# Rotary embedding on one Trainium2 core: sine and cosine products of both halves in one VectorE instruction each, and a shorter f32 tail on SyncE's queue

## Chip, cores, metric

One core of a Trainium2 chip. The metric is the device time of one execution, in us; the median of several executions is quoted. Single runs of one kernel scatter by some 0.1 to 0.3 us (a few lay 0.3 to 0.5 us above the median), so differences under 0.1 us are not read as differences. The experiments were run in five sets, each on one chip with the kernel before beside it: e1 to e4, e5 to e8, a1 to a4, f1 to f4, g1 and g2. The profiled executions quoted here were all fast, granted clock 1.0. A ratio is the mean time of one kernel's fast runs over that of the other's fast runs of the same rounds; it is therefore not quite the ratio of the medians. "The span" is from the profile's first instruction to its last; the time is some 1.8 us longer.

## The reference

```python
# x: (8, 8, 1024, 64) f32, freqs: (32,) f32, positions: (1024,) int32
half = x.shape[-1] // 2
angles = np.outer(positions, freqs)
cos, sin = np.cos(angles), np.sin(angles)
x_first, x_second = x[..., :half], x[..., half:]
out_first = x_first * cos - x_second * sin
out_second = x_first * sin + x_second * cos
```

In all 16.8 MB of f32 are read and 16.8 MB of f32 written.

## The kernel before

x is cut into eight tiles of 128 partitions x 64 rows x 64 columns. GpSimd's queue (q0 in the profile) loads them, f32 to bf16, all but the first 16 rows of the first tile, which SyncE's queue (q1) loads; later q0 stores each result, bf16 to f32. The last 24 rows of the last tile are computed straight to f32 and stored by q1 in three pieces of eight rows, so that the end of the program does not hang on q0 alone.

```python
for g in range(ntiles):                         # all loads are queued at the start
    lo = 0 if g else head
    nc.gpsimd.dma_start(out=xts[g][:, lo:], in_=hbm(x, g, lo))
# ... angles, sin_h and cos_h as bf16 [128, 64, 32] (cut) ...

def rotate(g, lo, hi, ot):
    xf = xts[g][:, lo:hi, :half];  xs = xts[g][:, lo:hi, half:]
    of = ot[:, :, :half];          os_ = ot[:, :, half:]
    sin = sin_h[:, lo:hi];         cos = cos_h[:, lo:hi]
    t1 = tpool.tile([P, C, half], bf16, name="t1")[:, :hi - lo]
    t2 = tpool.tile([P, C, half], bf16, name="t2")[:, :hi - lo]
    v.tensor_mul(out=t1, in0=xf, in1=sin)
    v.tensor_mul(out=t2, in0=xs, in1=sin)
    v.tensor_mul(out=of, in0=xf, in1=cos)
    v.tensor_mul(out=os_, in0=xs, in1=cos)
    v.tensor_sub(out=of, in0=of, in1=t2)
    v.tensor_add(out=os_, in0=os_, in1=t1)

tail = 3 * piece                                # piece = 8 rows
for g in [1, 0] + list(range(2, ntiles)):       # eight bf16 tiles, the last one without its tail
    hi = C if g < ntiles - 1 else C - tail
    ot = opool.tile([P, C, d], bf16, name="ot")[:, :hi]
    rotate(g, 0, hi, ot)
    ots.append(ot)
    nc.gpsimd.dma_start(out=hbm(out, g, 0, hi), in_=ot)
last = singles.tile([P, tail, d], f32)
rotate(ntiles - 1, C - tail, C, last)

for done in [pos_i, fr, x0] + ots[:-1]:         # SyncE waits here until each store but the last has landed
    sp.clobber_nop(outs=[sp.lower_ap(done)])
for r in range(0, tail, piece):                 # then issues the tail
    lo = C - tail + r
    tc.keep_in_program_order(
        sp.dma_start(out=hbm(out, ntiles - 1, lo, lo + piece), in_=last[:, r:r + piece]))
sp.clobber_nop(outs=[sp.lower_ap(ots[-1])])     # and waits for the last store
# ... and for the tail's pieces (cut) ...
```

## Time and profile before

| | before |
|---|---|
| time, median of the rounds with the changed kernel | 85.25 us |
| span | 83.6 us |
| VectorE busy | 63.5 us in 66 instructions |
| VectorE's last instruction ends | 73.7 us |
| tile 6 landed, tail issued | 77.8 us |
| first tail packet on q1 | 79.44 us |
| last landing on q0, on q1 | 80.80, 82.69 us |

The table reads from top to bottom in time: VectorE is done ten microseconds before the end, and what follows is waiting for bytes. The last two rows come from the trace's records of DMA packets and landings. The prediction shows the lines that this rests on.

### The profile page before, as it was taken

How to read it: one execution, taken by the hardware profiler on the slowest of the kernel's cores; microseconds unless marked ns; L12 is line 12 of the kernel's file. 1: busy time of each engine (PE TensorE's matmuls, PEld its weight loads, DVE VectorE, ACT ScalarE, POOL GpSimd, SP SyncE). 2: the span in 40 equal slices, each digit the busy share in tenths (PEclk: the TensorE clock that was granted, in tenths of full speed). 3: DMA queues.
4: the chain of work that ended last, by engine and by line, in shares of the span. 5: the costliest groups of instructions: out<-in, count | busy, mean ns of one | idle time of the engine just before them, and what ended most of it. 6: DMA issues, size and time to landing. Idle time of an engine off the chain costs nothing.

```text
span 83.6 us, 163 instructions
## 1 busy us (share of the span) xinstructions
DVE 63.5 (76%) x66; ACT 9.3 (11%) x6; POOL 8.7 (10%) x20
## 2 busy tenths in 40 slices
DVE  1024995089999999999999999999999999920000
ACT  0000049999000000000000000000000000000000
POOL 4960000000002001002002002000100202000000
DMA  0899999999999999999999999999999999999992
GB/s 0 182 202 259 227 208 227 204 227 208 212 220 208 227 208 227 204 212 223 200 388 423 423 455 400 470 388 463 408 439 439 416 455 423 455 392 422 431 331 70
DMA packets 3065, 25.45 MB, mean 304 GB/s; under 512 B 360, under 2 KB 376, under 8 KB 1144
## 3 DMA queue, kind: packets, MB, share of 16 engines
q0 software_dynamic: 2304, 24.12, 94.2%
q1 hardware_dynamic: 720, 1.31, 5.1%
q10 hardware_dynamic: 40, 0.01, 0.0%
q14 instruction: 1, 0.01, 0.0%
HBM read 16.79 MB, written 16.78 MB: 402 GB/s over the span
## 4 chain that ended last, share of the span: by engine, by line
DVE 67%; DMA 12%; ACT 7%; DVEq 1%; SPq 1%; issue 0%; ACTq 0%
DMA x<-in_x_dram 12%; DVE t L114 11%; DVE t L115 11%; DVE ot L119 10%; DVE ot L117 10%; DVE ot L116 10%; DVE ot L118 10%; ACT sin_h L96 2%; ACT L96 2%; ACT L101 2%; ACT xt L101 1%; DVEq L170 1%; DVE last L117 1%; DVE last L118 1%; DVE last L116 1%; SPq L56 1%
## 5 line engine op out<-in xcount | busy, mean ns | idle before, releaser
L114 DVE TENSOR_TENSOR t<-xt,sin_h 128x2048 bf16<-128x2048 bf16 (+2 forms) x9 | 9.9, 1099 | 3.5 <-ACT sin_h L96 3.5
L128 POOL DMA_DIRECT2D out_dram<-ot x8 | 4.2, 526 | 60.4 <-DVE ot L119 60.4
L115 DVE TENSOR_TENSOR t<-xt,sin_h 128x2048 bf16<-128x2048 bf16 (+2 forms) x9 | 9.9, 1099 | 0.0
L117 DVE TENSOR_TENSOR ot<-xt,cos_h 128x2048 bf16<-128x2048 bf16 (+1 forms) x8 | 9.3, 1167 | 0.0
L119 DVE TENSOR_TENSOR ot<-ot,t 128x2048 bf16<-128x2048 bf16 (+1 forms) x8 | 9.3, 1167 | 0.0
L116 DVE TENSOR_TENSOR ot<-xt,cos_h 128x2048 bf16<-128x2048 bf16 (+1 forms) x8 | 9.3, 1166 | 0.0
L118 DVE TENSOR_TENSOR ot<-ot,t 128x2048 bf16<-128x2048 bf16 (+1 forms) x8 | 9.3, 1166 | 0.0
L74 POOL DMA_DIRECT2D xt<-in_x_dram x8 | 4.3, 577 | 0.8 <-PEq L170 0.8
L76 DVE LOAD_MASK_SELECT pos_i<-pos_i x1 | 0.0, 14 | 3.8 <-DMA pos_i<-in_positions_dram 3.8
L101 ACT ACT_TABLE_LOAD x1 | 1.3, 1283 | 11.5 <-DMA x<-in_x_dram 11.5
L87 DVE TENSOR_TENSOR turns<-pos_f,fturn 128x2048 f32<-128x2048 f32 x1 | 2.3, 2293 | 0.0
L93 DVE TENSOR_TENSOR turns<-turns,whole 128x2048 f32<-128x2048 f32 x1 | 2.3, 2293 | 0.0
L99 ACT ACTIVATE cos_h<-whole,half_pi 128x2048 bf16<-128x2048 f32 x1 | 2.0, 2003 | 0.0
L96 ACT ACTIVATE sin_h<-turns 128x2048 bf16<-128x2048 f32 x1 | 1.9, 1909 | 0.0
L98 ACT ACTIVATE whole<-turns 128x2048 f32<-128x2048 f32 x1 | 1.9, 1893 | 0.0
L77 DVE LOAD_MASK_SELECT fr<-fr x1 | 0.0, 14 | 1.9 <-DMA fr<-in_freqs_dram 1.9
L96 ACT ACT_TABLE_LOAD x1 | 1.3, 1283 | 0.0
L91 DVE TENSOR_SCALAR whole<-turns 128x2048 f32<-128x2048 f32 x1 | 1.2, 1226 | 0.0
L101 ACT CAST xt<-x 128x1024 bf16<-128x1024 f32 x1 | 1.0, 1045 | 0.0
L117 DVE TENSOR_TENSOR last<-xt,cos_h 128x768 f32<-128x768 bf16 x1 | 0.9, 950 | 0.0
L119 DVE TENSOR_TENSOR last<-last,t 128x768 f32<-128x768 f32 x1 | 0.9, 950 | 0.0
L116 DVE TENSOR_TENSOR last<-xt,cos_h 128x768 f32<-128x768 bf16 x1 | 0.9, 949 | 0.0
(12 smaller groups left out, 2.6 us busy)
## 6 DMA issues: line engine op xcount, KB each, us to landing
out_dram<-ot POOLq DMA_DIRECT2D x7, 2048.0 KB, 18.5
xt<-in_x_dram POOLq DMA_DIRECT2D x7, 1024.0 KB, 25.2
out_dram<-ot POOLq DMA_DIRECT2D x1, 1280.0 KB, 11.2
xt<-in_x_dram POOLq DMA_DIRECT2D x1, 768.0 KB, 7.6
out_dram<-last SPq DMA_DIRECT2D x3, 256.0 KB, 3.6
x<-in_x_dram SPq DMA_DIRECT2D x2, 256.0 KB, 6.9
pos_i<-in_positions_dram ACTq DMA_DIRECT2D x1, 8.0 KB, 3.7
fr<-in_freqs_dram ACTq DMA_DIRECT2D x1, 0.5 KB
```

What stands on the lines that cost most here:

```text
L74: nc.gpsimd.dma_start(out=xts[g][:, lo:], in_=hbm(x, g, lo))
L87: nc.vector.tensor_mul(out=turns, in0=pos_f.to_broadcast([P, C, half]), in1=fturn.to_broadcast([P, C, half]))
L93: nc.vector.tensor_sub(out=turns, in0=turns, in1=whole)
L96: nc.scalar.activation(out=sin_h, in_=turns, func=Sin, scale=twopi)
L101: nc.scalar.copy(out=xts[0][:, :head], in_=x0)
L114: v.tensor_mul(out=t1, in0=xf, in1=sin)
L115: v.tensor_mul(out=t2, in0=xs, in1=sin)
L116: v.tensor_mul(out=of, in0=xf, in1=cos)
L117: v.tensor_mul(out=os_, in0=xs, in1=cos)
L118: v.tensor_sub(out=of, in0=of, in1=t2)
L119: v.tensor_add(out=os_, in0=os_, in1=t1)
L128: nc.gpsimd.dma_start(out=hbm(out, g, 0, hi), in_=ot)
```

## The change

The intent: fewer VectorE instructions, since sine (and cosine) multiply both halves alike and can be read twice through a repeated row; and eight rows fewer for the f32 tail, whose queue was taken to be the slower one.

```diff
     def rotate(g, lo, hi, ot):
-        ... six instructions, as above ...
+        n = hi - lo
+        pair = [P, n, 2, half]
+        xt = xts[g][:, lo:hi].rearrange("p c (two h) -> p c two h", two=2)
+        ot = ot.rearrange("p c (two h) -> p c two h", two=2)
+        t = tpool.tile([P, C, 2, half], bf16, name="t")[:, :n]
+        v.tensor_mul(out=t, in0=xt, in1=sin_h[:, lo:hi, None, :].to_broadcast(pair))
+        v.tensor_mul(out=ot, in0=xt, in1=cos_h[:, lo:hi, None, :].to_broadcast(pair))
+        v.tensor_sub(out=ot[:, :, 0], in0=ot[:, :, 0], in1=t[:, :, 1])
+        v.tensor_add(out=ot[:, :, 1], in0=ot[:, :, 1], in1=t[:, :, 0])
 
-    tail = 3 * piece
+    tail = 2 * piece
 ...
-    for done in [pos_i, fr, x0] + ots[:-1]:
+    for done in [x0, pos_i, fr] + ots[:-1]:
```

## The prediction

> **What bounds the kernel now.** I read the page first, then the stretches of time, the timeline of the end, the DMA traffic of the last microseconds, and the groups of instructions by shape. The page offers two candidates: the chain that ended last gives VectorE 67% of the span, and the slices show VectorE full from 17 us to 74 us. But the DMA row under it is full for longer:
>
> ```profile
> DVE  1024995089999999999999999999999999920000
> ...
> DMA  0899999999999999999999999999999999999992
> ...
> q0 software_dynamic: 2304, 24.12, 94.2%
> q1 hardware_dynamic: 720, 1.31, 5.1%
> ...
> HBM read 16.79 MB, written 16.78 MB: 402 GB/s over the span
> ```
>
> VectorE is full in the middle only; DMA is full from the second slice to the last but one, and two queues together fill 99% of what sixteen engines have. The same by stages (columns after the stretch: length, then busy us of VectorE, ScalarE, GpSimd with instruction counts, clock, DMA share, GB/s):
>
> ```profile
> 2.00:42.00 40.00, 31.61 (x31) 9.32 (x6) 5.14 (x10) 1.00 1.02 215
> 42.00:77.80 35.80, 31.73 (x33) 0.00 (x0) 2.61 (x5) 1.00 1.06 428
> 77.80:80.40 2.60, 0.00 (x0) 0.00 (x0) 0.00 (x0) 1.00 1.04 397
> 80.40:82.40 2.00, 0.00 (x0) 0.00 (x0) 0.00 (x0) 1.00 0.73 251
> 82.40:83.60 1.20, 0.00 (x0) 0.00 (x0) 0.00 (x0) 1.00 0.00 0
> ```
>
> Until 42 us the loads run. The 215 GB/s count what lands as bf16; the f32 read from HBM is twice that, 430 GB/s. From 42 us to 77.8 us the stores run at 428 GB/s. Both are the same ceiling. Only after 80.4 us does the DMA share fall (0.73, then 0); that is the only place where time is left. The timeline says who waits for whom there:
>
> ```profile
> 65.20 0.52 POOL L128 DMA_DIRECT2D out_dram<-ot  x1 [6.29 <-DVE ot L119]
> ...
> 69.61 0.52 POOL L128 DMA_DIRECT2D out_dram<-ot  x1 [3.89 <-DVE ot L119]
> ...
> 72.78 0.95 DVE L119 TENSOR_TENSOR last<-last,t 128x768 f32<-128x768 f32 x1
> 77.84 2.27 SPq L141 DMA_DIRECT2D out_dram<-last  x3
> ```
>
> The last two bf16 stores are handed to GpSimd's queue at 65.2 and 69.6 us, but the stores move one after another, and SyncE, which waits for each to land, counts 4.8 us between them (2.1 MB in 4.8 us is again some 430 GB/s). Tile 6 lands at 77.8 us, so its bytes began near 73: about 7 us after it was ready. The last bf16 store waits 8 us. VectorE itself is done at 73.7 us, 10 us before the end of the span. The chain's 67% VectorE is therefore a chain of order, not of need. The f32 tail is ready at 73.7 us, but SyncE issues it only at 77.84 us, after its wait for tile 6. Its transfer looks like this (two stretches, 77.8 to 79.4 and 79.4 to 80.4 us):
>
> ```profile
> q0 software_dynamic: 68, 0.70, 110.5%
> ```
> ```profile
> q1 hardware_dynamic: 149, 0.28, 77.1%
> q0 software_dynamic: 21, 0.05, 17.2%
> ```
>
> For 1.6 us after the issue no tail packet moves; q0 has the engines. When q1 begins, q0 has 0.05 MB left, so almost all of the 0.79 MB tail moves alone, from 79.4 to 82.35 us: 266 GB/s, not 430. Its three pieces land 3.6 us after their issues, at 81.4, 82.1 and 82.7 us by the trace's landing records (0.63 us apart); q0's last landing is 80.8 us. The tail's third piece ends the program.
>
> **What the Trainium skill says.** (1) "VectorE: DVE Perf Modes", § The perf-mode tier table: a bf16 `tensor_tensor` runs two elements a cycle, f32 one; 1224 and 2293 ns for 2048. The trace agrees: 1217 ns and 2293 ns. (2) "Vector Engine (DVE) Microarchitecture Reference", § 5.1: the two-element mode asks for 16-bit operands and an innermost step of one, and a row read again and again with a step of 0 still ran in that mode with two sources. The strided halves, rows of 32, do run at 1217 ns here; no instruction here repeats a bf16 row. (3) "DMA: Bandwidth & Descriptors", § Where 436 GB/s comes from: 435 GB/s for one core's DMA. The trace's 428 to 430 is close to that. (4) Same page, § Queues, rings and completion order: each engine takes turns between queues, packet by packet. The trace shows both queues' packets between 79.4 and 80.4 us, too few of q0 to test it.
>
> **The change part by part.** *VectorE's instructions.* The costs come from these groups:
>
> ```profile
> L114 DVE TENSOR_TENSOR t<-xt,sin_h 128x2048 bf16<-128x2048 bf16 x7 | 8.5, 1217 | 3.5 <-ACT sin_h L96 3.5
> L116 DVE TENSOR_TENSOR last<-xt,cos_h 128x768 f32<-128x768 bf16 x1 | 0.9, 949 | 0.0
> L118 DVE TENSOR_TENSOR ot<-ot,t 128x1280 bf16<-128x1280 bf16 x1 | 0.8, 816 | 0.0
> ```
>
> Neighbours overlap by 0.08 us, so I use the steps between starts: 1.137 us at 2048 elements (six take 51.19 to 58.01), 0.735 us at 1280 (six take 64.82 to 69.23). The slope is 0.402 us over 768 = 0.523 ns an element; the fixed part 0.066 us. One f32 step at 768 is 0.87 us: (0.87 - 0.066)/768 = 1.047 ns an element.
> - Full tile: before 6 x 1.137 = 6.82 us. After: two products of 4096 at 2.21 us, add and subtract at 1.137: 6.69 us. Saved 0.13 us, two fixed parts, times seven = 0.9 us. A product should show some 2290 ns (1217 + 2048 x 0.523).
> - Last bf16 part, 48 rows in place of 40: 2 x 1.67 + 2 x 0.87 = 5.08 us, before 4.41: +0.67 us.
> - f32 tail, 16 rows in place of 24: 0.60 + 1.14 + 2 x 0.60 = 2.94 us, before 4.42 (69.23 to 73.65): -1.48 us.
> - Sum: -0.9 + 0.67 - 1.48 = -1.7 us of VectorE, which ends at 72.0 us; its instructions fall from 66 to 48. The last store is ready at 69.3 - 0.9 + 0.67 = 69.1 us.
>
> All this lies beside the DMA stream, inside 7 to 8 us of slack. On the path it is worth zero.
>
> *The split of the end.* The bytes stay the same. Eight rows (128 x 8 x 64 x 4 B = 0.262 MB) move from q1 to q0. SyncE's issue time doesn't change, since tile 6 lands as before. Bounds for the gain:
> - If the pace of the pieces sets the end, the third one's 0.63 us goes: -0.63 us.
> - If the queues' rates set it: from 79.4 us q0 has 0.05 + 0.26 = 0.31 MB at 430 GB/s, 0.73 us, then q1's 0.524 MB at 266 GB/s, 1.97 us; together 2.70 us against 2.95 us now: -0.25 us. Any mixing of the two queues in that time makes it better.
>
> The middle is -0.45 us. *The new order of SyncE's waits* touches waits that are over by 20 us, long before 77.8 us: zero. Total 85.27 - 0.45 = 84.8 us.
>
> **Rivals.**
> - *VectorE is the bound*, as the chain suggests: then the 1.7 us would come through whole, 83.6 us. Against it: VectorE's tail sits ready 4 us before its issue, and DMA is full before and after VectorE's end.
> - *The repeated sine row drops VectorE to one element a cycle.* Then a product is 4096 x 1.047 ns + 0.066 = 4.35 us, a tile 11.0 us; seven tiles from 17.1 us, then 8.3 us and 3.5 us for the last one's two parts, end at 106 us, and some 5 us of transfer and 1.7 us outside the span follow: about 112 us. The skill's rule and the fast strided rows speak against it; that none here repeats a bf16 row leaves it a small chance.
> - *The end is bound by bytes, not by the queue*: the sixteen engines finish together whatever the split, and what q1 loses, q0 gains: 85.2 us. For it: DMA share still 1.04 to 80.4 us. Against it: 0.73 after, with q1 alone.
> - *q0's last store becomes the last to land*: its 80.8 us plus 0.61 us (0.26 MB at 430) plus its turns with q1 is 81.4 to 82 us, still under 82.7. It caps the gain near 0.7 us.
>
> **Range and chances.** 84.8 us, with 84.4 (a little past the 0.63 us bound) to 85.4 (no gain and some noise; the three runs of before lie within 0.1 us). Two per cent faster would be below 83.6 us, more than all idle DMA after 80.4 us can give short of a perfect end: 0.02. Slower by two per cent needs the lost mode or a surprise in the queues: 0.035. The rest, 0.945, is within.
>
> **What would show it.** Product groups of 128x4096 at about 2290 ns (4300 to 4400 ns: mode lost); VectorE's last instruction ending near 72 us; DMA full without a gap from 2 to 80 us; tile 6 landing, and so the first tail issue, within 0.2 us of 77.8; two tail issues; q0 busy to some 80.2 to 81 us beside q1; the last landing 0.25 to 0.65 us earlier. The prediction is wrong if the tail's issue moves by more than that, if DMA's rate in the store stage changes though the bytes don't, or if a tail piece, sharing with q0, lands later than 3.6 us after its issue by more than the piece saved.

## The result

85.14 us (85.09 to 85.21, four runs) against 85.25 us (85.20 to 85.32): ratio 0.9987, interval 0.9970 to 1.0004. The change is worth 0.1 us, about the scatter, and the interval takes in no change at all; 0.45 us had been forecast.

The page of the changed kernel, its slices and its queues:

```profile
DVE  1023996079999999999999999999999999500000
...
DMA  0799999999999999999999999999999999999991
...
q0 software_dynamic: 2304, 24.38, 95.0%
q1 hardware_dynamic: 576, 1.05, 3.8%
```

VectorE's full stretch ends one slice earlier; the DMA row does not move. What left q1 (5.1% to 3.8%) came to q0 (94.2% to 95.0%). The same stretches of time as shown of before (length; busy us of VectorE, ScalarE, GpSimd; clock, DMA share, GB/s):

```profile
2.00:42.00 40.00, 31.59 (x24) 9.32 (x6) 5.14 (x10) 1.00 1.02 215
42.00:77.80 35.80, 30.09 (x22) 0.00 (x0) 2.61 (x5) 1.00 1.06 428
77.80:80.40 2.60, 0.00 (x0) 0.00 (x0) 0.00 (x0) 1.00 1.04 406
80.40:82.40 2.00, 0.00 (x0) 0.00 (x0) 0.00 (x0) 1.00 0.62 225
82.40:83.60 1.20, 0.00 (x0) 0.00 (x0) 0.00 (x0) 1.00 0.00 0
```

VectorE is 1.6 us less busy between 42 and 77.8 us, and the stores still run at 428 GB/s: nothing of it reaches the end. The largest group of VectorE instructions by shape:

```profile
L112 DVE TENSOR_TENSOR t<-xt,sin_h 128x4096 bf16<-128x4096 bf16 x7 | 15.9, 2283 | 3.4 <-ACT sin_h L97 3.4
```

2283 ns for 4096 elements is the two-element mode with the repeated row (f32 takes 2293 ns for 2048 in the same trace); 2290 had been forecast. The timeline of the end:

```profile
65.95 0.52 POOL L124 DMA_DIRECT2D out_dram<-ot  x1 [5.62 <-DVE ot L115]
...
69.96 0.52 POOL L124 DMA_DIRECT2D out_dram<-ot  x1 [3.49 <-DVE ot L115]
...
71.44 0.68 DVE L115 TENSOR_TENSOR last<-last,t 128x512 f32<-128x512 f32 x1
77.39 1.23 SPq L137 DMA_DIRECT2D out_dram<-last  x2
```

VectorE ends at 72.1 us, 1.6 us earlier, and the tail is issued when tile 6 has landed, at 77.4 us, in two transfers. VectorE's pace and end are as forecast. Two steps are not. The prediction let tile 6 land within 0.2 us of 77.8 us and called a larger shift a sign of being wrong: the issue came 0.45 us earlier (77.39 against 77.84), and 0.40 us of that is one late DMA engine. Before, the last of the sixteen engines landed tile 6 0.51 us behind the fifteenth, here 0.11 us. (Why is taken up under the merged products.) And the last bf16 store was ready at 69.7 us, not 69.1, since the tail's sine product ran before its last two instructions; it still waited for its turn on q0. The DMA traffic from the issue to 80.0 us, and from there to the last packet:

```profile
q0 software_dynamic: 94, 1.16, 111.2%
```
```profile
q1 hardware_dynamic: 288, 0.52, 69.1%
q0 software_dynamic: 16, 0.00, 2.0%
```

For 2.7 us after its issue no tail packet moves; before, it was 1.6 us. The tail's start is not tied to its issue but to the end of q0's last store, and that has grown by the eight rows: first tail packet at 80.10 us against 79.44, +0.66 us. q1's share of the work has shrunk by one piece, and it ends at 82.49 us against 82.69.

### The profile page after: what moved, and what is told of

Same layout as the page of the kernel before. It is cut to its first block, busy times and chain, and to the rows that moved or that the text cites. A ratio compares the mean times of both kernels' runs of the same rounds, so it can differ in the third digit from the quotient of the medians.

```text
span 83.4 us, 149 instructions
## 1 busy us (share of the span) xinstructions
DVE 61.9 (74%) x48; ACT 9.3 (11%) x6; POOL 8.7 (10%) x20
## 4 chain that ended last, share of the span: by engine, by line
DVE 53%; issue 13%; DMA 12%; ACT 7%; SPq 1%; DVEq 1%; ACTq 0%
DVE ot L113 20%; DMA x<-in_x_dram 12%; DVE t L112 11%; DVE ot L115 11%; DVE ot L114 8%; ACT sin_h L97 2%; ACT L97 2%; ACT L102 2%; DVE last L113 1%; ACT xt L102 1%; DVE last L114 1%; SPq L56 1%; DVEq L166 1%; ACTq L102 0%
## 5 line engine op out<-in xcount | busy, mean ns | idle before, releaser
L112 DVE TENSOR_TENSOR t<-xt,sin_h 128x4096 bf16<-128x4096 bf16 (+2 forms) x9 | 18.3, 2046 | 3.4 <-ACT sin_h L97 3.4
L113 DVE TENSOR_TENSOR ot<-xt,cos_h 128x4096 bf16<-128x4096 bf16 (+1 forms) x8 | 17.6, 2214 | 0.0
L88 DVE TENSOR_TENSOR turns<-pos_f,fturn 128x2048 f32<-128x2048 f32 x1 | 2.3, 2293 | 0.0
L94 DVE TENSOR_TENSOR turns<-turns,whole 128x2048 f32<-128x2048 f32 x1 | 2.3, 2293 | 0.0
L113 DVE TENSOR_TENSOR last<-xt,cos_h 128x1024 f32<-128x1024 bf16 x1 | 1.2, 1214 | 0.0
L114 DVE TENSOR_TENSOR last<-last,t 128x512 f32<-128x512 f32 x1 | 0.7, 692 | 0.0
L115 DVE TENSOR_TENSOR last<-last,t 128x512 f32<-128x512 f32 x1 | 0.7, 684 | 0.0
```

The costliest lines, as they stand in the source:

```text
L88: nc.vector.tensor_mul(out=turns, in0=pos_f.to_broadcast([P, C, half]), in1=fturn.to_broadcast([P, C, half]))
L94: nc.vector.tensor_sub(out=turns, in0=turns, in1=whole)
L112: v.tensor_mul(out=t, in0=xt, in1=sin_h[:, lo:hi, None, :].to_broadcast(pair))
L113: v.tensor_mul(out=ot, in0=xt, in1=cos_h[:, lo:hi, None, :].to_broadcast(pair))
L114: v.tensor_sub(out=ot[:, :, 0], in0=ot[:, :, 0], in1=t[:, :, 1])
L115: v.tensor_add(out=ot[:, :, 1], in0=ot[:, :, 1], in1=t[:, :, 0])
```

## The experiments

The theories, as they stood at first. A: VectorE is off the path, and the split's gain is eaten by q0, since the tail runs after q0 and not beside it. B: the split wins what was forecast and the merged products give it back. All kernels of the sets gave correct results. Columns: tail in transfers x rows; the ratio is to the kernel before in the same set; then, from one profile each, first tail packet, last landing on q0 and on q1, us.

| run | VectorE | tail | us (before) | ratio, 95% interval | first | q0 | q1 |
|---|---|---|---|---|---|---|---|
| before | six | 3x8 | 85.25 | 1 | 79.44 | 80.80 | 82.69 |
| changed kernel | merged | 2x8 | 85.14 (85.25) | 0.9987, 0.9970-1.0004 | 80.10 | 80.98 | 82.49 |
| a1_after_again | merged | 2x8 | 85.23 (85.35) | 0.9981, 0.9966-0.9996 | 80.20 | 81.18 | 82.60 |
| e1_split_only | six | 2x8 | 85.37 (85.38) | 1.0000, 0.9988-1.0012 | 79.99 | 81.30 | 82.60 |
| e2_vector_only | merged | 3x8 | 85.22 (85.38) | 0.9984, 0.9972-0.9996 | 79.55 | 80.52 | 82.53 |
| g1_vector_only_again | merged | 3x8 | 85.21 (85.31) | 0.9985, 0.9973-0.9998 | 79.44 | 80.46 | 82.48 |
| e3_early_issue | merged | 2x8, early | 85.16 (85.38) | 0.9979, 0.9967-0.9990 | 79.12 | 81.32 | 82.45 |
| e4_tail8 | merged | 1x8 | 84.97 (85.38) | 0.9953, 0.9939-0.9967 | 80.71 | 81.76 | 82.26 |
| e5_no_tail | merged | none | 85.71 (85.41) | 1.0043, 1.0029-1.0056 | - | 82.33 | - |
| a2_tail32 | merged | 4x8 | 85.63 (85.35) | 1.0040, 1.0018-1.0062 | 79.01 | 80.06 | 83.05 |
| e6_tail48 | merged | 6x8 | 87.50 (85.41) | 1.0248, 1.0235-1.0262 | 78.77 | 78.66 | 84.73 |
| a3_one_piece | merged | 1x16 | 84.78 (85.35) | 0.9931, 0.9916-0.9945 | 79.98 | 81.06 | 82.29 |
| f3_one_piece16_again | merged | 1x16 | 85.00 (85.31) | 0.9960, 0.9941-0.9979 | 80.35 | 81.28 | 82.50 |
| g2_one_piece12 | merged | 1x12 | 84.84 (85.31) | 0.9942, 0.9928-0.9955 | 80.44 | 81.62 | 82.40 |
| f1_one_piece24 | merged | 1x24 | 85.05 (85.31) | 0.9969, 0.9952-0.9987 | 79.64 | 80.58 | 82.55 |
| f2_before_one_piece24 | six | 1x24 | 85.39 (85.31) | 1.0006, 0.9990-1.0022 | 79.67 | 80.74 | 82.78 |
| e7_pad_count | merged + 24 tiny | 2x8 | 85.32 (85.41) | 0.9992, 0.9980-1.0004 | 80.14 | 81.35 | 82.65 |
| e8_pad_time | merged + 2.27 us | 2x8 | 85.39 (85.41) | 1.0001, 0.9989-1.0013 | 80.09 | 81.11 | 82.55 |
| a4_pad_time_again | merged + 2.27 us | 2x8 | 85.35 (85.35) | 0.9998, 0.9985-1.0012 | 80.08 | 80.98 | 82.46 |
| f4_pad_time_double | merged + 4.5 us | 2x8 | 85.14 (85.31) | 0.9979, 0.9959-0.9998 | 80.16 | 81.14 | 82.65 |

### One part of the change at a time

The split alone (edit of the kernel before), the merged products alone (edit of the changed kernel, run twice), and the whole change once more:

```diff
-    tail = 3 * piece          # e1: kernel before
+    tail = 2 * piece
-    tail = 2 * piece          # e2, g1: changed kernel
+    tail = 3 * piece
```

> Before's six VectorE instructions a tile, with only the tail cut to 16 rows. Theory A (VectorE lies off the path; what the whole change won, 0.11 us, is the split's): 85.1 us, ratio to before 0.998 to 1.000, as the whole change. Theory B (the split wins the 0.45 us forecast and the merged products give 0.3 us back): 84.8 us, ratio 0.995. In both VectorE's last instruction ends about 73 us, and two tail issues. Theory A also expects the first tail packet only at about 80.0 us, after the last packets of q0, as in the changed kernel (80.05), not at 79.4.

> The merged products with the tail left at 24 rows. Theory A (VectorE off the path): 85.25 us, ratio to before 0.999 to 1.001, though VectorE is 0.9 us less busy and ends about 72.8 us. Theory B (the merged products cost something that hides the split's gain): 85.5 us, ratio 1.003 or more. A third, that VectorE binds: 84.4 us. The first tail packet at 79.4 us as before.

> The changed kernel itself once more, beside the other three of this set. If its first result holds (0.9987): ratio to before 0.9975 to 1.000. The mechanism from the runs so far: first tail packet within 0.1 us of 80.1, last landing 82.4 to 82.6, 0.85 to 0.95 us from there to the end of the span.

> Merged products with the old tail of three pieces, again. If 2.98 us was typical: 2.9 to 3.1 us from first tail packet to last landing, ratio to before 0.9975 to 0.9995, so the split is worth nothing on top. If 3.25 was: 3.15 to 3.3 us, last landing near 82.75, ratio 0.9995 to 1.001, and the split is worth some 0.15 us.

The split alone is worth nothing: 1.0000 with the old products (within 0.1 us). With the merged ones, 16 rows gave 0.9987 and 0.9981, and 24 rows 0.9984 and 0.9985. Theory B falls, since the merged products cost nothing. A holds for the split, but not in its detail that the split had brought the 0.11 us: the small gain, 0.15% or 0.13 us, follows the merged products, with two pieces as with three. (With one transfer of 24 rows it may be larger, see below. The new order of SyncE's waits went with the merged products in every run and was not tested alone.)

The profiles say where the split's gain went. With 24 rows the first tail packet came at 79.44, 79.55 and 79.44 us; with 16 rows in two pieces, issued late, at 79.99 to 80.20, mean 80.11 of seven. So q0 took 0.63 us for the eight rows. From there to the last landing three pieces took 3.25, 2.98 and 3.04 us, mean 3.09; two pieces took 2.38 to 2.60, mean 2.46. So q1 was rid of 0.63 us. The two cancel.

### Does q1 run beside q0, if it is issued early?

```diff
-    for done in [x0, pos_i, fr] + ots[:-1]:
-        sp.clobber_nop(outs=[sp.lower_ap(done)])
     ... the two tail issues ...
-    sp.clobber_nop(outs=[sp.lower_ap(ots[-1])])
+    for done in [x0, pos_i, fr] + ots:
+        sp.clobber_nop(outs=[sp.lower_ap(done)])
```

> The changed kernel with SyncE's waits for the bf16 stores moved behind the tail's two issues, so that they go out when VectorE is done, at about 72 us and not at 77.4. Theory A (the tail moved alone after q0 because it was issued when only some 5 packets an engine of q0 were left, all ahead of it; while more of q0 is queued the queues take turns, as they did for the second piece of x at 5 to 10 us): the tail's packets start between 73 and 76 us among q0's, all are through before 81 us, q0 ends last near 81.4 us, at the 430 GB/s of both; 84.2 to 84.7 us, ratio to before 0.988 to 0.993. Theory B (q1 gets nothing while q0 has stores queued, whenever it is issued): first tail packet near 80 us again, 85.1 us. Theory C (turns are taken but q1's small packets cost as much time beside q0 as alone): 85.0 us with the end on q0.

The time is 85.16 us: no gain over the changed kernel. The line of the timeline, then the DMA traffic from 73 to 79 us, then from 79 to 80.4 us:

```profile
72.56 1.23 SPq L135 DMA_DIRECT2D out_dram<-last  x2
```
```profile
q0 software_dynamic: 196, 2.58, 106.9%
```
```profile
q0 software_dynamic: 38, 0.47, 80.6%
q1 hardware_dynamic: 40, 0.08, 20.7%
```

Issued at 72.6 us, the tail moved its first packet at 79.1 us: 6.6 us later, while some ten packets of q0 passed on each engine (in the 5.3 us from 1.25 us after the issue; the delay with an idle q0 is the run with six pieces, below). Then the queues moved as many packets one as the other, 40 against 38, as they would by turns. In these 1.4 us the two together moved 392 GB/s, less than the 431 of q0 alone just before. Theory A of the expectation (start between 73 and 76 us, 84.2 to 84.7 us) is refuted. The result lies between B and C: both queues move, but late, and they win nothing; the end stays on q1 (82.45 us), not on q0 as C had it. The forecast's "any mixing makes it better" is refuted on both counts: at a late issue there is no mixing, and with mixing there is no gain.

### The length of the tail

```diff
-    tail = 2 * piece
+    tail = piece              # e4; 4 * piece in a2, 6 * piece in e6; no tail at all in e5
```

> The changed kernel with a tail of one piece, 8 rows. Theory A (serial: each 8 rows moved cost q0 0.61 to 0.65 us and save q1 0.75 to 1.0 us): first tail packet at about 80.6 us, the one piece through by about 81.8 us, time 84.8 to 85.05. Theory B (only bytes count): 85.14, the same as the changed kernel within 0.1. Theory C (the piece's fixed way from issue to landing now dominates, so nothing more is won): 85.2 or more.

> The changed kernel without any f32 tail: all eight stores are whole bf16 tiles on GpSimd's queue, SyncE stores nothing. Theory D (a row costs nearly the same on either queue, 0.61 us per 8 rows on q0 and some 0.65 on q1, and only the second queue's start and drain, some 0.3 us, come on top): q0's last data near 81.8 us, last landing 82.1 to 82.3, time 84.7 to 84.95. Theory A (8 rows on q1 cost 0.97 us, 0.36 more than on q0): 84.6 or less. Theory E (q0's own end is slower than the tail's): 85.2 or more.

> The changed kernel with a tail of 32 rows, four pieces. From the first tail packet to the last landing the runs so far took 1.55 us for one piece, 2.4 to 2.6 for two, 3.0 to 3.25 for three, 6.0 for six. Theory D (a further piece costs q1 0.63 us and saves q0 0.6): first packet near 78.95 us, last landing near 82.65, ratio to this set's changed kernel 1.000 to 1.002. Theory A (0.97 us a piece on q1): last landing near 83.0, ratio 1.004 to 1.006. Should the start be held by the way from issue to first packet, 1.25 us in the run with six pieces, there is an idle gap before it; at 77.4 + 1.25 = 78.65 it should not be.

> The changed kernel with a tail of 48 rows, six pieces; VectorE is still done before tile 6 lands. The forecast's rate for q1, 266 GB/s as an average over start, run and drain, taken as the price of each row: 8 rows cost 0.97 us there and 0.61 on q0, so four pieces more cost 4 x 0.36 = 1.4 us: 86.5 us. Theory D (in its run q1 moves 390 to 416 GB/s, as the pieces land 0.63 us apart; 0.05 us for each 8 rows): 4 x 0.05 = 0.2 us, 85.3 to 85.4 us, landings of the pieces 0.62 to 0.67 us apart.

One piece of 8 rows is better (0.9953), none is worse (1.0043), four and six pieces are worse (1.0040, 1.0248). From first tail packet to last landing: 1.55 us for one piece, 2.46 for two, 3.09 for three, 4.03 for four, 5.96 for six. Theory D, an even 0.63 us a piece, fits only the step from three to two; the others cost 0.9 to 1.0 us each, about what theory A says. In the long tails many 2 KB packets took over 120 ns in place of 84: 100 of 512 and 151 of 768, against 7 to 31 of 384, 5 to 14 of 256 and none of 128. No run here tells why. So eight rows happened to cost the same on both queues at the one step that the change takes.

Six pieces show a second limit. Their issue line, and the DMA records of 78.28 to 78.76 us:

```profile
77.53 3.84 SPq L137 DMA_DIRECT2D out_dram<-last  x6
```
```profile
DMA packets 0, 0.00 MB, mean 0 GB/s; under 512 B 0, under 2 KB 0, under 8 KB 0
```

q0 has run dry and q1's first packet comes at 78.77 us, 1.24 us after its issue: the DMA engines stand still for half a microsecond. Waiting for tile 6 leaves too little on q0 here to cover the way of the tail from its issue to its first packet.

No tail shows the third. Its last landing, 82.33 us, is earlier than the changed kernel's 82.49, yet its span is 0.4 us longer. SyncE's waits at the very end, of the kernel without a tail and of the changed kernel (us in total, times, longest):

```profile
SPq L156 <- PEq L156: 1.2, 2, 0.7
```
```profile
SPq L166 <- PEq L166: 0.6, 2, 0.5
```

From the last landing to the end of the span it is 1.44 us in this run, the only one in which GpSimd's queue lands last, and 0.86 to 0.96 us in all runs in which SyncE's does. So the tail on SyncE's queue saves some 0.5 us at the very end; no run tells why. Theory D's 84.7 us for no tail failed mostly on this.

### One transfer in place of pieces

```diff
-    for r in range(0, tail, piece):
+    for r in range(0, tail, tail):          # a3, f3: 16 rows; g2: 12; f1: 24; f2: the kernel before
         lo = C - tail + r
-            sp.dma_start(out=hbm(out, ntiles - 1, lo, lo + piece), in_=last[:, r:r + piece]))
+            sp.dma_start(out=hbm(out, ntiles - 1, lo, lo + tail), in_=last[:, r:r + tail]))
```

> The changed kernel with its 16 tail rows issued as one transfer, so that a packet may be 4 KB in place of 2. Theory P (the small packets are what makes q1 slow): from first tail packet to last landing 2.0 to 2.2 us in place of 2.4 to 2.6, ratio to this set's changed kernel 0.995 to 0.998. Theory S (start, drain and receipt of the queue are what it costs, not the packet size): 2.4 to 2.6 us as with two pieces, ratio 0.999 to 1.001.

> The best so far, merged products with 16 tail rows in one transfer, beside the 24-row ones: 0.993 to before, between 0.9915 and 0.9945 as in its first set.

> Merged products, tail of 24 rows in one transfer (6 KB a row). Bytes cost the same on both queues: the same as one transfer of 16 rows within 0.1 us, first tail packet near 79.5, last landing 82.2 to 82.4, ratio to before 0.993 to 0.995. If the forecast's step holds for an uncut tail (q1 dearer by 0.25 us or more for 8 rows): 0.996 to 0.998.

> The kernel before, all as it was, but its 24 tail rows in one transfer. If the cutting into three pieces was the cost and VectorE lies off the path: the same as the merged kernel with one transfer of 24 rows within 0.1 us, 0.993 to 0.995 to before. If the merged products are worth 0.14 us of their own: 0.9945 to 0.997, and 0.0015 above the merged one.

> Merged products with 12 tail rows in one transfer (3 KB a row), between the 8 rows (0.9953) and the 16 rows (0.9931 and 0.9960) in one transfer. First tail packet near 80.45, q0's last landing 81.4, q1's last 82.2 to 82.35; ratio to before 0.992 to 0.996. Above 0.997 would mean that rows of 3 KB cost more than rows of 2 or 4 KB.

The DMA issues of the kernel with 16 rows in one transfer:

```profile
out_dram<-last SPq DMA_DIRECT2D x1, 512.0 KB, 4.8
```

(f1 also sets `tail = 3 * piece` and g2 `tail = 12`; the waits for earlier pieces, which one transfer doesn't have, are taken out.)

From the first tail packet to the last landing it took 2.31 and 2.15 us, two pieces 2.46. Its packets are 4 KB and took 159 ns, hence 412 GB/s over sixteen engines; the 2 KB packets of the pieces took 84 ns at best, 390 GB/s. It is the best kernel, with the 12-row one: 84.78 and 85.00 us, ratios 0.9931 and 0.9960, and 0.9942 for 12 rows; both of its intervals lie below 1.

Theory P has the direction right, with less in the first profile than it said (2.0 to 2.2 us). The repeat missed its own expectation (0.9915 to 0.9945). One transfer of 24 rows gave 0.9969 with the merged products. That is 0.0009 or 0.08 us above 16 rows of the same set, but each interval is some 0.15 us wide on either side, and the other set's 16 rows lie 0.0038 below. By its ratio to before it even falls where its expectation had the forecast's step hold for an uncut tail. What the split is worth with one transfer therefore stays open. With the old products one transfer of 24 rows gave 1.0006, no better than three pieces: the number of transfers alone does not explain the gain either. Beside one transfer the merged products were thus worth 0.0037, or 0.3 us, where f2's expectation had 0.0015 and the pieces had shown 0.0015. The noise of the two runs, some 0.0024 together, leaves room for both.

### Why the merged products win anything

> The changed kernel with 24 tiny VectorE copies (two elements a partition, into a tile that nobody reads) spread over the tiles, so VectorE has 70 instructions again and is still done before tile 6 lands. Theory F (with many instructions, VectorE's program is longer and an 8 KB load of instructions falls into the stores, as at 55.4 us before; the DMA engine that carries it is late from then on, and that is where the change's 0.1 us came from): the instruction packet is there between 40 and 70 us, from the next store on the sixteenth landing is 0.45 to 0.6 us behind the fifteenth, and the time is 85.25 to 85.4 us. Theory G (the load is of another engine's making, and the late engine chance): no packet, the sixteenth landing 0.1 us behind, 85.14 us.

> The control for the padded count: the changed kernel with two useless VectorE products of 2048 elements, 2.27 us more VectorE time but only two instructions. Theory A and F (VectorE's time lies off the path): 85.14 us, no instruction packet before the end, sixteenth landing 0.1 us behind the fifteenth. If VectorE's time did count: 85.14 + 2.3 = 87.4 us.

> The changed kernel with 2.27 us of useless VectorE work, again, now on the same chip as the changed kernel. If VectorE's time is off the path: ratio to this set's changed kernel 0.999 to 1.001, last landing 82.4 to 82.6. If its 85.39 us of the earlier set was a real cost: 1.002 to 1.004.

> The changed kernel with four useless VectorE products, 4.5 us more VectorE time; its last store is then ready about 74 us, still 3 us before its turn on q0 comes. A real price of VectorE time (0.15 us for 2.27): ratio to before 1.0012 to 1.003. Chance, or a price of any such extra at all: 0.998 to 1.0005. No instruction packet among the stores.

```diff
         rotate(g, 0, hi, ot)
+        for _ in range(3):                                   # e7
+            v.tensor_copy(out=pad[:, 0, :2], in_=ot[:, 0, :2])
+        if g == 3:                                           # e8, a4; g in (3, 5) in f4
+            v.tensor_mul(out=pad, in0=ot[:, :, :half], in1=cos_h)
+            v.tensor_mul(out=pad, in0=ot[:, :, :half], in1=cos_h)
```

VectorE's time is not it, as far as the runs can tell: 4.5 us more gave 0.9979, no slower than the changed kernel. Two runs with 2.27 us more had looked like a price (1.0001, 0.9998), but their spans, 83.43 and 83.33 us, are those of the changed kernel (83.39 and 83.48). Their extra 0.15 us lies outside the span: time less span is 1.96 and 1.98 us in them, 1.82 and 1.86 in the changed kernel.

The same measure cuts the other way for 4.5 us: time less span is only 1.72 us there. The record has the span of every execution, to 0.1 us, and their means less those of before in the same set are fairer: -0.23 us for the changed kernel (a1), -0.22 and -0.15 with three pieces (e2, g1), -0.18 and -0.22 with 2.27 us more (e8, a4), and -0.08 with 4.5 us more (f4), each to some 0.1 us. So 2.27 us cost nothing within the span, and 4.5 us perhaps 0.1 us; what lies outside the span is not explained.

What does differ is one packet. The queues from 54 to 57 us, of the kernel before, of the changed kernel, and of the changed kernel with 24 tiny copies:

```profile
q0 software_dynamic: 79, 1.28, 105.1%
q14 instruction: 1, 0.01, 0.7%
```
```profile
q0 software_dynamic: 78, 1.28, 104.3%
```
```profile
q0 software_dynamic: 78, 1.28, 105.0%
q14 instruction: 1, 0.01, 0.7%
```

An 8 KB load of instructions falls among the stores. It is there in all four kernels with 66 or 72 VectorE instructions (before, e1, f2; e7 has 72, not the 70 of its expectation) and in none of those with 44 to 52. In those with 48 to 52 a packet of the same kind and size comes after the end of the span, at 84.3 to 86.8 us; without a tail (44) the trace shows none.

From the next store on, the last of the sixteen engines lands 0.3 to 0.6 us behind the fifteenth in the first three, where it had been 0.05 to 0.1 us, and 0.25 to 0.3 us in e7, where it had been 0.2 us already (0.45 to 0.6 had been expected). In the others that lag is mostly 0.15 us or less, but up to 0.3 in four of them (a1, a2, f4, g2). Adding instructions brings the packet back, so that part of theory F is shown. That the packet costs the 0.13 us is supported only. The four kernels with it have ratios of 0.9992 to 1.0006, and mean spans of -0.06 to +0.04 us to before, against -0.15 to -0.23 in the kernels above without it (a1, e2, g1, e8, a4); but f4, without the packet, has -0.08. By time, e7 is not told apart from e8.

## Why the prediction was wrong

- *DMA is the bound, VectorE off the path:* right. VectorE ended 1.6 us earlier (1.7 forecast) and at most 0.1 us came of it; useless work of 4.5 us cost nothing in time, and in span perhaps 0.1 us.
- *The repeated row keeps the two-element mode:* right, 2283 ns for 4096 bf16 elements, as "Vector Engine (DVE) Microarchitecture Reference" of the Trainium skill, § 5.1, had it.
- *q0 pays 0.61 us for the eight rows:* right, 0.63. But of the 1.6 us from issue to first packet, read as "q0 has the engines", some 1.24 us would have passed anyway: in the run with six pieces they passed though q0 ran dry.
- *Tile 6 lands as before:* wrong by 0.45 us, 0.40 of it through the late engine. It did not matter, since the first packet waits for q0.
- *"then q1's 0.524 MB at 266 GB/s, 1.97 us; together 2.70 us against 2.95 us now":* this is the step that failed. It let q1 save 0.98 us; q1 saved 0.63. The 266 GB/s is an average over the start, the run and the drain of three pieces in one profile, and it was used as the price of the piece that left. Moreover, this profile was on the long side (85.36 us): counted to the last landing, three pieces took 3.25 us there, and 2.98 and 3.04 in two other kernels. With 0.63 for 0.98 the sum is 0.63 - 0.63 = 0, which is what the split measured. That the figure fits other steps better (16 to 8 rows 0.91 us, 24 to 32 rows 0.94) does not save it here; why this step was cheaper is open.
- *The other bound, "the pace of the pieces sets the end", -0.63 us:* wrong. The first piece's start was taken to stay, but it follows q0's last store and moved by as much.
- *"Any mixing ... makes it better":* wrong, by the early issue. These two led to a middle of 0.45 us, where the rival "the end is bound by bytes" had 85.2 us. Its number came true partly by luck: what q1 lost q0 did gain at this step, but not "whatever the split", as 8 rows (0.9953) and 48 rows (1.0248) show.
- *Merged products are worth zero:* not quite. They carry the 0.13 us that were measured, for which the instruction load is a likely, not a proven, cause.
- *A slip of reading:* tile 6's bytes began about 7.8 us after its hand-over by the prediction's own numbers (65.2 and 73), not 7. Nothing rests on it.

Open are why packets of long tails are slow, the exact price of the instruction load, whether the merged products gain more beside one transfer, and what makes the time outside the span differ by up to 0.3 us between kernels.

## What to carry to other kernels

Where two DMA queues share the engines and the second starts as the first runs out, moving bytes between them wins only the difference of their marginal costs; take that from two transfers of different size, not from bytes over time of one. Compute that was done five microseconds before its bytes' turn was worth at most 0.1 us here, however full its row looked. Before a small gain is explained, see whether it lies inside the span. Of the things tried at the end of this kernel, the number of transfers in the tail did more than their split: one of 8, 12 or 16 rows with merged products gave 0.4 to 0.7% over the kernel before, and with the old products one of 24 rows gave nothing.

## What the Trainium skill lacked or had wrong

- "DMA: Bandwidth & Descriptors", § Queues, rings and completion order: the page has each engine take turns, a packet at a time, and drain a packet of several descriptors whole. Equal numbers were seen once both queues moved (40 against 38), but only 6.6 us after the second one's issue, while some ten records of the first passed on each engine. The page gives no time for such a wait; whether a record of the trace is a packet of the page or one descriptor, no run here shows.
- "Runtime: NRT & Kernel Launch", § Instruction fetch mechanics: it gives refills of 16 KiB blocks, mostly hidden. Here the load was one packet of 8192 bytes, at 55.4 us among the stores, after which one engine landed 0.4 to 0.6 us late.
- No page that I found has the end: 1.44 us from the last landing to the end of the span when GpSimd's queue lands last (one run), 0.86 to 0.96 us when SyncE's does.
- "DMA: Bandwidth & Descriptors", § Where 436 GB/s comes from: the prediction took 435 GB/s from it, a ceiling of the fabric, and left out that the section has the HBM side bind at about 358 GB/s for transfers between HBM and SBUF. The one core that ran here stored at 428 GB/s, so the measurement decides.
